# A second seven-product chunk in the first half of both output products of a decoder layer

## The chip, the cores and the metric

The kernel runs on one core of one Trainium2 chip. The metric is device time in microseconds (us) from start to end of the program. Engines are called PE (TensorE, the matmuls), DVE (VectorE), ACT (ScalarE), POOL (GpSimd) and SP (SyncE, which issues most of the transfers). Each of them runs its own list of instructions in the order of that list and waits where an operand is not there yet.

## The reference

One decoder layer on 256 tokens of width 2048, all in float32:

```python
h = h + 0.5 * swiglu(rmsnorm(h, g_ffn1), w1_gate, w1_up, w1_down)
z = rmsnorm(h, g_mix) @ w_in
y_a = spatial_gating(z[..., :2048], g_v, w_s, b_s)          # 1024 channels
y_b = window_attention_sinks(q, k, v, sinks)                # 1024 channels
y = concat(rmsnorm(y_a, g_a_out), rmsnorm(y_b, g_b_out))
h = h + y @ w_out
h = h + cross_attention(rmsnorm(h, g_x), rmsnorm(mem, g_mem), w_xq, w_xkv, w_xo)   # 4 heads x 512
h = h + 0.5 * swiglu(rmsnorm(h, g_ffn2), w2_gate, w2_up, w2_down)
out = rmsnorm(h, g_final)
```

The change touches the two output products, `y @ w_out` (called wo) and the last product of the cross attention, with `w_xo` (called xo). Each is (256 x 2048) by (2048 x 2048) and is added into the residual h.

## The kernel before, in words

**Chunks and units.** Every large product is cut into units of eight chunks. A unit makes 256 tokens x 1024 columns; a chunk is 256 of the 2048 rows of the weight, so a chunk is a 2x2 block product: two blocks of 128 tokens by two blocks of 128 rows (A11, A12, A21, A22), times two by two blocks of weight (B11 to B22, 128 x 512 each). wo and xo are two units each, a first half (columns 0 to 1023) and a second half. The eight chunks of a unit stand at places 0 to 7 in the order in which they are computed, and their sums stay in PSUM banks until the unit is done.

**Three matmuls for one product.** Each operand is split into a high and a low part (`split`, L146: ACT casts the high part, L147, and DVE subtracts it for the low part, L148). A product of two blocks is three matmuls: high x high, low x high, high x low. In every chunk but the first and the last of a unit the passes with the low part of the weight stand last (`passes`, L405).

**Kinds.** A plain chunk (N) has four sums of two block products: 24 matmuls, into the banks P2, Q3, R and Q4. A chunk of kind S replaces the eight block products by seven on sums of blocks (a Strassen-Winograd form): 21 matmuls, into P1, P2, Q3, Q5, Q7, Q6 and Q4. For it DVE and ACT make more: sums of the weight's blocks (L337, L340, L341: the tile named ...t), their high and low parts (...th, ...tl), and sums of the activations' blocks with their parts (L226, L231, L232). The tile names are those of the program: in wo, `wow` is a chunk's weight as loaded, `wowh` and `wowl` its two parts, `wot`, `woth`, `wotl` the sums; `yafh`/`yafl` and `ybfh`/`ybfl` are the parts of the activations (pairs 0 to 3 from y_a, 4 to 7 from y_b). In xo the pairs are `xofh`/`xofl`. `KINDS_O` says that pairs 3 and 5 carry the sums too. The extra banks of an S chunk (P1, Q5, Q6, Q7) come from the pool `trp` of four banks, which the transposes of side work use as well; P2, Q3, R and Q4 come from the pool `acc` of four, so that the next unit's P2, Q3, R and Q4 each wait until DVE has added the old one into h (`adds`, L614).

**Who orders the work.** PE's list is fixed by the program text (`PINNED`). DVE's, ACT's and SP's lists come from a scheduler at build time. Weights go through three buffers (`raw`), their parts through two (`wh`, `wl`), the sums through one (`t`, `th`, `tl`). `push` (L494) prepares a chunk's weight before the chunk ahead of it in the text is multiplied.

**Side work.** Smaller work is written as generators that advance by one step about every six matmuls (`side_step`), for example `y_pairs` (transposes that make the pairs of wo) and `attend_memory` (L1296, one per head: transposes of q, scores, softmax, transposes of the probabilities into `xpT`, their parts `xpTs`, and the products `xo` with the values, two per head; each product is split into one pair of xo). Head 2 makes pairs 4 and 5, head 3 makes pairs 6 and 7. When a chunk needs a pair that does not exist yet, `have` runs the side work to the end of that pair at once (`until`), so its instructions stand directly ahead of the chunk in PE's list. While an S chunk's extra banks are in use, from the first to the last S chunk of a unit, side work is held; ahead of the first S chunk `added_unit` makes all eight pairs.

After the last S chunk `early` adds P1, Q5, Q6 and Q7 into h on DVE; after the last chunk `late` adds P2, Q3, R and Q4. From the finished blocks of h the next norm takes its squares, and then its scaled rows and their transposes, in the second half of the same product.

## Time and profile before

| what | value |
|---|---|
| median of 3 runs | 2036.48 us (2033.58 to 2036.55) |
| the profiled execution's own time | 2033.63 us |
| its span, first to last instruction | 2031.9 us |
| granted TensorE clock, mean | 0.999 |
| PE, DVE, ACT busy share | 99%, 91%, 65% |
| wo (first half from 1045.6, second from 1090.8) | to 1134.9 us |
| xo (first half from 1235.8, second from 1293.2) | to 1338.8 us |

Times in views of the trace are microseconds from the start of the span. A matmul with 512 columns is listed with 0.39 us, though the next one starts sooner, since they are pipelined: distances between starts are what counts on PE. Likewise the next instruction on DVE or ACT may start up to 0.1 us before the listed end of the one ahead.

### The profile page before, as it was taken

Reading aid. Unit: us, or ns where it says so; the run is one execution under the profiler, and the core shown is the slowest. Engines: PE = TensorE matmul, PEld = TensorE weight load, DVE = VectorE, ACT = ScalarE, POOL = GpSimd, SP = SyncE. Lnnn points to the kernel's source line nnn. Section 1 sums busy time; section 2 is a strip of 40 time slices with the busy share of each in tenths; the row PEclk is TensorE's granted clock in tenths of the full one; section 3 lists DMA queues with packets and bytes.
Section 4 is the critical chain, followed back from the end, with each engine's and each line's share of the span. In section 5 each row is a group of like instructions: output and inputs, shape, how many; then the busy total and the mean of one; then the engine's idle time right before and its main releaser. Section 6 shows DMA issues by size and latency. Waiting matters only on the chain.

```text
span 2031.9 us, 24271 instructions
## 1 busy us (share of the span) xinstructions
PE 2015.5 (99%) x9203; PEld 1668.8 (82%) x9203; DVE 1853.6 (91%) x1994; ACT 1313.2 (65%) x1460; POOL 34.4 (2%) x57
## 2 busy tenths in 40 slices
PE   9999999999999999999999999999999999999998
PEld 7788888888888888888888888888888888888886
DVE  6999999999999978989879987899999999999998
ACT  7765566567665766755566666676656666676664
POOL 0000000000000010200000000000000000000000
PEclk9999999999999999999999999999999999999999
DMA  8666666666556575544675544556566656665563
GB/s 312 197 206 225 215 218 205 236 209 220 196 191 219 177 252 178 202 166 166 208 227 182 198 160 145 187 187 224 197 239 215 215 205 231 214 219 206 187 228 125
DMA packets 115333, 415.83 MB, mean 205 GB/s; under 512 B 61824, under 2 KB 63888, under 8 KB 68112
## 3 DMA queue, kind: packets, MB, share of 16 engines
q1 hardware_dynamic: 112768, 407.14, 57.6%
q0 software_dynamic: 2016, 6.30, 1.0%
q8 instruction: 72, 1.18, 0.2%
q10 hardware_dynamic: 432, 0.84, 0.1%
q14 instruction: 45, 0.37, 0.1%
HBM read 398.52 MB, written 2.10 MB: 197 GB/s over the span
## 4 chain that ended last, share of the span: by engine, by line
PE 85%; DVE 9%; issue 3%; ACT 2%; DMA 2%; SPq 0%; POOL 0%; POOLq 0%; DVEq 0%; ACTq 0%
PE f1gQ L428 12%; PE f2gQ L428 12%; PE f2dQ L428 6%; PE f1dQ L428 6%; PE f1gP L428 5%; PE f2gP L428 4%; PE xqQ L428 3%; PE f2dP L428 3%; PE f1dP L428 3%; PE woQ L428 2%; PE xoQ L428 2%; PE f2dR L428 2%; PE f1dR L428 2%; DVE f1gwl L148 2%; PE vQ L428 2%
## 5 line engine op out<-in xcount | busy, mean ns | idle before, releaser
L148 DVE TENSOR_TENSOR f1gwl<-f1gw,f1gwh 128x1536 fp32r<-128x1536 f32 (+2 forms) x94 | 181.6, 1934 | 24.5 <-ACT f1gwh L147 23.8
L147 ACT CAST f2gwh<-f2gw 128x1536 fp32r<-128x1536 f32 (+1 forms) x88 | 150.5, 1712 | 66.4 <-PE f2gQ L428 44.9
L148 DVE TENSOR_TENSOR f2gwl<-f2gw,f2gwh 128x1536 fp32r<-128x1536 f32 (+1 forms) x88 | 179.1, 2036 | 8.0 <-ACT f2gwh L147 8.0
L147 ACT CAST f1gwh<-f1gw 128x1536 fp32r<-128x1536 f32 (+2 forms) x94 | 153.1, 1629 | 45.0 <-PE f1gQ L428 19.3
L147 ACT CAST f1gth<-f1gt 128x1024 fp32r<-128x1024 f32 x76 | 79.9, 1051 | 103.1 <-DVE f1gt L337 68.7
L147 ACT CAST f2gth<-f2gt 128x1024 fp32r<-128x1024 f32 x82 | 85.4, 1050 | 64.2 <-DVE f2gt L341 34.0
L428 PE MATMUL f2gQ<-f2gwh,n4fh 128*128 128x512 f32 x317 | 123.8, 390 | 0.6 <-DVE f2gv L587 0.6
L428 PE MATMUL f2gQ<-f2gwh,n4fl 128*128 128x512 f32 x317 | 123.4, 389 | 0.0
L428 PE MATMUL f1gQ<-f1gwh,n1fl 128*128 128x512 f32 x286 | 111.4, 390 | 1.7 <-DVE n1fl L148 1.7
L428 PE MATMUL f1gQ<-f1gwh,n1fh 128*128 128x512 f32 x286 | 111.6, 390 | 0.0
L147 ACT CAST f2dwh<-f2dw 128x2048 fp32r<-128x2048 f32 (+1 forms) x44 | 77.4, 1758 | 47.5 <-PE f2dQ L428 39.5
L147 ACT CAST f1dwh<-f1dw 128x2048 fp32r<-128x2048 f32 (+1 forms) x44 | 77.3, 1757 | 43.7 <-PE f1dQ L428 42.7
L148 DVE TENSOR_TENSOR f1dwl<-f1dw,f1dwh 128x2048 fp32r<-128x2048 f32 (+1 forms) x44 | 92.0, 2092 | 12.0 <-ACT f1dwh L147 11.8
L148 DVE TENSOR_TENSOR f2dwl<-f2dw,f2dwh 128x2048 fp32r<-128x2048 f32 (+1 forms) x44 | 92.0, 2091 | 11.2 <-ACT f2dwh L147 11.1
L148 DVE TENSOR_TENSOR f2gtl<-f2gt,f2gth 128x1024 fp32r<-128x1024 f32 x82 | 99.5, 1218 | 1.0
L428 PE MATMUL f2gQ<-f2gwl,n4fh 128*128 128x512 f32 x317 | 96.7, 389 | 0.0
L148 DVE TENSOR_TENSOR f1gtl<-f1gt,f1gth 128x1024 fp32r<-128x1024 f32 x76 | 92.2, 1216 | 0.5
L428 PE MATMUL f1gQ<-f1gwl,n1fh 128*128 128x512 f32 x286 | 86.9, 389 | 0.0
L428 PEld LDWEIGHTS f2gQ<-f2gwh,n4fh 128*128 128x128 f32 x317 | 59.5, 188 | 13.8 <-DVE f2gv L587 1.6
L428 PEld LDWEIGHTS f2gQ<-f2gwh,n4fl 128*128 128x128 f32 x317 | 59.5, 188 | 12.2
L428 PEld LDWEIGHTS f2gQ<-f2gwl,n4fh 128*128 128x128 f32 x317 | 59.4, 188 | 12.3
L428 PE MATMUL f2gP<-f2gwh,n4fh 128*128 128x512 f32 x176 | 68.6, 390 | 0.0
(824 smaller groups left out, 6072.2 us busy)
## 6 DMA issues: line engine op xcount, KB each, us to landing
f2gw<-in_w_gu SPq DMA_DIRECT2D x88, 1024.0 KB, 4.9
f1gw<-in_w_gu SPq DMA_DIRECT2D x86, 1024.0 KB, 4.8
f1dw<-in_w_down SPq DMA_DIRECT2D x44, 1024.0 KB, 4.8
f2dw<-in_w_down SPq DMA_DIRECT2D x44, 1024.0 KB, 4.8
wow<-in_w_out SPq DMA_DIRECT2D x16, 1024.0 KB, 4.8
xqw<-in_w_xq SPq DMA_DIRECT2D x16, 1024.0 KB, 4.8
xow<-in_w_xo SPq DMA_DIRECT2D x16, 1024.0 KB, 4.8
qw<-in_w_in SPq DMA_DIRECT2D x8, 1024.0 KB, 4.8
```

The costliest lines, as they stand in the source:

```text
L147: nc.scalar.copy(hi, src)
L148: nc.vector.tensor_tensor(lo, src, hi.bitcast(F32), ALU.subtract)
L428: nc.tensor.matmul(self.banks[name], x, y, start=name not in self.begun, stop=self.left[name] == 0)
```

## The change

In the first half of wo and of xo, chunk 3, whose pair carries the sums anyway, becomes a chunk of kind S beside chunk 5, and the chunks stand in other orders: in wo 0, 1, 2, 4, 5, 6, 3, 7 (S at places 4 and 6), in xo 0, 1, 2, 4, 6, 5, 7, 3 (S at places 5 and 7). Before, both had the order 0 to 7 with S at place 5 alone. The second halves stay as they are. Since xo's first half now ends on an S chunk, its `early` runs inside `late`, and the squares of all four blocks come after all adds.

```diff
-    HALVES_O = ("NNNNNSNN", "NNNSNSNN")
+    HALVES_O = {
+        ("wo", 0): ("NNNNSNSN", (0, 1, 2, 4, 5, 6, 3, 7)),
+        ("xo", 0): ("NNNNNSNS", (0, 1, 2, 4, 6, 5, 7, 3)),
+        ("wo", 1): ("NNNSNSNN", range(8)),
+        ("xo", 1): ("NNNSNSNN", range(8)),
+    }
...
-        def early(u):
+        def early(u, at_once=False):
...
-            if on_block is None:
+            if at_once:
+                rest()
+            elif on_block is None:
...
-        def late(u, blocks=range(TB)):
+        def late(u, blocks=range(TB), also=None):
             for name, tb, j in BLOCKS:
                 if tb in blocks:
                     add(hb(tb, j), u[name], tb, j)
-                    if on_block is not None:
+                    if on_block is not None and also is None:
                         on_block(j0 + j, tb)
+            if also is not None:
+                also(u, True)
+                for name, tb, j in BLOCKS:
+                    on_block(j0 + j, tb)
...
     def added_unit(s, w, cb, pairs, on_block):
-        kinds = HALVES_O[cb]
+        kinds, order = HALVES_O[s, cb]
         u = Unit(s, kinds, LATE_O, clear=True)
...
             push(
-                u, i, w[i, cb],
-                lambda i=i: (have(pairs, 7 if i == kinds.index("S") else i), pairs[i])[1],
-                lambda i=i: early(u) if i == kinds.rindex("S") else end(u) if i == last else None,
+                u, i, w[order[i], cb],
+                lambda i=i: (have(pairs, 7 if i == kinds.index("S") else order[i]), pairs[order[i]])[1],
+                lambda i=i: (
+                    end(u, also=early if kinds[last] == "S" else None) if i == last
+                    else early(u) if i == kinds.rindex("S") else None
+                ),
             )
```

The lists of the engines show more than the diff. Three places follow; a row has the line, the operation, what it writes from what it reads (with the tile's number), and its shape.

DVE in the first half of wo, before: the weight splits of places 2 and 3, then the low part of pair 4 (`ybfl_8581`, in two pieces) and the weight split of place 4.

```order
L148 TENSOR_TENSOR wowl_8529<-wow_8527,wowh_8528 128x2048
L148 TENSOR_TENSOR wowl_8559<-wow_8557,wowh_8558 128x2048
L142 SCALAR_TENSOR_TENSOR ybfl_8581<-yb_8575,sm,ybfh_8580 128x256
L337 TENSOR_TENSOR wot_8674<-wow_8670 128x1024
L142 SCALAR_TENSOR_TENSOR ybfl_8581<-yb_8575,sm,ybfh_8580 128x256
L148 TENSOR_TENSOR wowl_8631<-wow_8629,wowh_8630 128x2048
```

The same stretch of DVE's list after the change, down to the low part of pair 5's sums (`ybfl_8600`):

```order
L337 TENSOR_TENSOR wot_8633<-wow_8629 128x1024
L148 TENSOR_TENSOR wowl_8529<-wow_8527,wowh_8528 128x2048
L148 TENSOR_TENSOR wowl_8559<-wow_8557,wowh_8558 128x2048
L340 TENSOR_TENSOR wot_8633<-wot_8633,wow_8629 128x512
L142 SCALAR_TENSOR_TENSOR ybfl_8581<-yb_8575,sm,ybfh_8580 128x256
L341 TENSOR_TENSOR wot_8633<-wot_8633,wow_8629 128x512
L148 TENSOR_TENSOR wotl_8640<-wot_8633,woth_8639 128x1024
L142 SCALAR_TENSOR_TENSOR ybfl_8581<-yb_8575,sm,ybfh_8580 128x256
...
L340 TENSOR_TENSOR wot_8717<-wot_8717,wow_8713 128x512
L148 TENSOR_TENSOR wowl_8684<-wow_8682,wowh_8683 128x2048
L148 TENSOR_TENSOR ybfl_8600<-ybf_8604,ybfh_8599 128x512
```

The sums of the weight at place 4 now stand around the splits of places 2 and 3 and between the two pieces of pair 4's low part, while pair 4 is read one chunk earlier, at place 3. The low part of pair 5's sums stands behind the split of place 5's weight (`wowl_8684`); on ACT its high part stands behind that weight's cast in the same way, as these rows of ACT's list after the change show:

```order
L147 CAST woth_8643<-wot_8633 128x1024
L147 CAST ybfh_8597<-ybr_8601 128x512
L147 CAST wowh_8683<-wow_8682 128x2048
L147 CAST ybfh_8599<-ybf_8604 128x512
L141 ACTIVATE ybfh_8623<-yb_8618,sm 128x256
```

Before, the cast ahead of `ybfh_8599` was that of the S chunk itself, and the chunk that reads the result stood one place later.

DVE at the turn from the first to the second half of wo, after the change. Ahead of these rows stand the adds of P2 and Q5 into h; the last row is the add of Q4, the fourth bank of the pool `acc`, and the weight split ahead of it belongs to place 1 of the second half:

```order
L645 TENSOR_TENSOR h<-h,woz_8784 128x512
L626 SCALAR_TENSOR_TENSOR h<-woQ_1682_8465,h 128x512
L626 SCALAR_TENSOR_TENSOR h<-woR_8466,h 128x512
L646 TENSOR_TENSOR h<-h,woz_8784 128x512
L148 TENSOR_TENSOR wowl_8844<-wow_8842,wowh_8843 128x2048
L626 SCALAR_TENSOR_TENSOR h<-woQ_1684_8467,h 128x512
```

Before, all four of these adds stood ahead of that split.

PE in the first half of xo, before: the last matmul of place 2, head 2's four transposes, then 18 matmuls of place 3 (the first two and the last two shown) and the first of twelve products with the values.

```order
L428 MATMUL xoQ_2007_10090<-xowl_10147,xofh_10006 128x512 x2
L1332 MATMUL xpT_10309<-ident,pr_10223 128x128 x4
L428 MATMUL xoP_2004_10087<-xowh_10241,xofh_10036 128x512
L428 MATMUL xoP_2004_10087<-xowh_10241,xofl_10037 128x512
...
L428 MATMUL xoP_2004_10087<-xowl_10242,xofh_10036 128x512 x2
L169 MATMUL xo_10342<-xpTs_10314,mvh_10230 128x256
L169 MATMUL xo_10342<-xpTs_10315,mvh_10230 128x256
```

The same place after the change:

```order
L428 MATMUL xoQ_2012_10099<-xowl_10156,xofh_10015 128x512 x2
L1346 MATMUL xpT_10318<-ident,pr_10232 128x128 x4
L169 MATMUL xo_10333<-xpTs_10323,mvh_10239 128x256
L169 MATMUL xo_10333<-xpTs_10324,mvh_10239 128x256
...
L428 MATMUL xoP_2009_10096<-xowh_10250,xofh_10346 128x512
L428 MATMUL xoP_2009_10096<-xowh_10250,xofl_10347 128x512
```

The twelve products now stand directly behind the transposes, and place 3, which has become chunk 4, reads their result (`xofh_10346`, `xofl_10347`) directly behind them. For head 3 the same happens once more at place 4 (chunk 6): six matmuls stand between its transposes and its products, which were twelve before, and the chunk that reads the first result follows at once.

## The prediction

> **What bounds the kernel now.** I read the page first, then PE's waits, then the two stretches that the change touches.

> ```profile
> span 2031.9 us, 24271 instructions
> PE 2015.5 (99%) x9203; PEld 1668.8 (82%) x9203; DVE 1853.6 (91%) x1994; ACT 1313.2 (65%) x1460; POOL 34.4 (2%) x57
> ```

> PE is busy for all but 16 us. The waits of PE in the whole trace are few; the longest are these (waiter, line, releaser, total, times, longest):

> ```profile
> PE f1gQ L428 <- DVE n1fl L148: 1.7, 1, 1.7
> PE xoQ L428 <- ACT n4r L266: 1.2, 1, 1.2
> ```

> One of them, 1.2 us, lies in xo. In the windows of the two first halves (length, then busy time of PE, PEld, DVE and ACT) PE never waits at all:

> ```profile
> 1045.00:1091.00 46.00, 46.00 (x214) 38.11 (x213) 36.66 (x42) 28.92 (x35) 0.00 (x0) 1.00 0.64 196
> 1235.00:1293.00 58.00, 58.00 (x314) 49.85 (x312) 46.83 (x59) 37.66 (x56) 0.00 (x0) 1.00 0.38 135
> ```

> So PE sets the time in both: a matmul less is a gain of one distance between starts, and any new wait of PE is a loss in full. DVE and ACT have free time there, but on average only; what counts is when a given tile is ready.

> **What is removed.** PE's rows in wo give the distance and the places where chunks 4 and 5 start:

> ```profile
> 1064.50 0.40 PE L428 MATMUL woP<-wowh,yafl 128*128 128x512 f32 x1
> 1069.76 0.39 PE L428 MATMUL woP<-wowh,ybfh 128*128 128x512 f32 x1
> 1071.35 0.39 PE L428 MATMUL woQ<-wowh,ybfl 128*128 128x512 f32 x1
> 1075.20 0.39 PE L428 MATMUL woP<-wowh,ybfh 128*128 128x512 f32 x1
> 1076.79 0.39 PE L428 MATMUL woQ<-wowh,ybfl 128*128 128x512 f32 x1
> ```

> 1069.76 to 1071.35 are seven distances: 0.227 us each. Two chunks lose three matmuls each (24 become 21): 6 x 0.227 = **1.4 us gained**. Everything else is a question of lateness.

> **wo, place 3: pair 4 is wanted a chunk earlier and made later.** Its second low piece is needed by the fourth matmul of place 3, which starts at 1064.50 above. DVE's list now begins the stretch with the weight sum of place 4, and that weight must have landed. It is issued by SP and lands 6.5 us later (the list of transfers of that window):

> ```profile
> 1051.19 0.53 SPq L358 DMA_DIRECT2D wow<-in_w_out  x1
> wow<-in_w_out SPq DMA_DIRECT2D x1, 1024.0 KB, 6.5
> ```

> SP's list is unchanged, so it lands at 1057.7 again. Behind it DVE has eight instructions up to that piece. Their durations, on DVE before:

> ```profile
> 1056.05 4.49 DVE L148 TENSOR_TENSOR wowl<-wow,wowh 128x2048 fp32r<-128x2048 f32 x2 [2.07 <-ACT wowh L147]
> 1064.07 1.23 DVE L337 TENSOR_TENSOR wot<-wow 128x1024 f32<-128x1024 f32 x1 [2.72 <-DMA wow<-in_w_out]
> 1065.21 0.48 DVE L142 SCALAR_TENSOR_TENSOR ybfl<-yb,sm,ybfh 128x256 fp32r<-128x256 f32 x1
> 1065.60 2.28 DVE L148 TENSOR_TENSOR wowl<-wow,wowh 128x2048 fp32r<-128x2048 f32 x1
> 1069.75 0.69 DVE L341 TENSOR_TENSOR wot<-wot,wow 128x512 f32<-128x512 f32 x1
> 1070.35 1.22 DVE L148 TENSOR_TENSOR wotl<-wot,woth 128x1024 fp32r<-128x1024 f32 x1
> ```

> 1.23 + 2 x 2.28 + 0.69 + 0.48 + 0.69 + 1.22 + 0.48 = 9.35, less seven overlaps of 0.08 (two splits of 2.28 take 4.49): 8.8 us, so the piece is ready at 1066.5. **Place 3 loses 2.0 us.** If the weight landed before 1056.0, DVE could do the first sum in its 2.07 us of idle time, and 0.3 would be left; if DVE's list were late by one more operation of 0.7, 2.7.

> **wo, place 4: the S chunk is one place earlier.** Its eighth matmul is the first that reads the low part of pair 5's sums; by the rows above it comes 1.59 us after the chunk's start (1075.20 to 1076.79). Place 4 would start at 1069.76 + 2.0 = 1071.8, so it is due at 1073.4. On ACT the high part now stands behind a full weight cast, which waits until PE has left place 3's weight:

> ```profile
> 1061.28 1.91 ACT L147 CAST wowh<-wow 128x2048 fp32r<-128x2048 f32 x1 [0.45 <-PE woQ L428]
> 1068.14 1.49 ACT L147 CAST wowh<-wow 128x1536 fp32r<-128x1536 f32 x1 [1.25 <-PE woQ L428]
> ```

> PE released it at 1068.14; with the 2.0 that is 1070.1, and the cast ends at 1072.0. DVE then has the split of the same weight (2.28, to 1074.3) and the low part of 512 columns (0.69): 1074.95. **Place 4 loses 1.6 us.** It is 0 if the order on ACT costs nothing, and 2.5 if DVE starts 0.9 later.

> **wo, turn to the second half: the fourth bank.** The second half starts here (PE), and DVE added Q4 and split the next weight thus:

> ```profile
> 1090.84 0.39 PE L428 MATMUL woP<-wowh,yafh 128*128 128x512 f32 x1
> 1091.04 0.69 DVE L621 SCALAR_TENSOR_TENSOR h<-woQ,h 128x512 f32<-128x512 f32 x1 [0.67 <-PE woQ L428]
> 1092.96 2.29 DVE L148 TENSOR_TENSOR wowl<-wow,wowh 128x2048 fp32r<-128x2048 f32 x1 [1.23 <-ACT wowh L147]
> ```

> With U the start of the second half, PE wants the Q4 bank after 18 matmuls, at U + 4.1. The add of Q4 now stands behind that split. The split waits for a cast of 1.91 that can start when PE leaves place 7's weight, at about U: it runs from U + 1.9 to U + 4.2, and the add ends at U + 4.9. **0.8 us lost**, between 0 (split elsewhere) and 1.5. The first half of wo thus costs 2.0 + 1.6 + 0.8 = 4.4 us.

> **xo, head 2: its products lose their cover.** PE, then DVE, then ACT, before:

> ```profile
> 1259.92 0.60 PE L1332 MATMUL xpT<-ident,pr 128*128 128x128 f32 x4
> 1260.27 0.48 PE L428 MATMUL xoP<-xowh,xofh 128*128 128x512 f32 x1
> 1264.48 1.59 PE L169 MATMUL xo<-xpTs,mvh 128*128 128x256 f32 x12
> 1265.91 0.63 PE L428 MATMUL xoQ<-xowl,xofh 128*128 128x512 f32 x2
> ...
> 1260.48 2.28 DVE L148 TENSOR_TENSOR xowl<-xow,xowh 128x2048 fp32r<-128x2048 f32 x1
> 1262.76 0.67 DVE L148 TENSOR_TENSOR xpTs<-xpT,xpTs 128x512 fp32r<-128x512 f32 x1
> 1263.87 2.35 DVE L148 TENSOR_TENSOR xotl<-xot,xoth 128x1024 fp32r<-128x1024 f32 x2
> 1266.73 0.69 DVE L148 TENSOR_TENSOR xofl<-xo,xofh 128x512 fp32r<-128x512 f32 x1 [0.51 <-ACT xofh L147]
> ...
> 1261.02 0.58 ACT L147 CAST xpTs<-xpT 128x512 fp32r<-128x512 f32 x1
> 1266.11 0.59 ACT L147 CAST xofh<-xo 128x512 fp32r<-128x512 f32 x1 [0.36 <-PE xo L169]
> 1268.93 0.78 ACT L1359 COPY xor<-xo 128x128 f32<-128x128 f32 x4 [2.23 <-PE xo L169]
> ```

> Up to the transposes nothing has moved. The 4.2 us from 1260.27 to 1264.48 were 18 matmuls of place 3, behind which the split of the probabilities was hidden. Now the products follow at 1260.27. The second of them, 0.12 later (twelve take 1.43 to the next start), reads the low part, which DVE ends at 1262.76 + 0.67 = 1263.43: **3.0 us lost**.

> The group ends 1.47 later, at 1264.9; ACT casts to 1265.5, DVE is in its two sums until 1266.2 (1263.87 + 2.35) and has the low part at 1266.8. The second matmul of place 3 would have started at 1265.0: **1.85 us lost**. Both rest on durations and positions that the trace has almost unchanged; I bound them by 2.4 to 3.2 and 1.2 to 2.2.

> **xo, head 3.** PE goes on with five matmuls, the second product of head 2 (1.43), twelve matmuls, four transposes (0.35) and six matmuls: head 3's second product is due at 1266.8 + 23 x 0.227 + 1.43 + 0.35 + 0.12 = 1273.9. On ACT, head 2's second product (over at 1269.5) starts a chain: four copies (0.78), a cast (0.6), a low part (0.69) and a difference on DVE and a second cast (1.5 together, an estimate from the 0.69 and the casts of 0.6), which is 1272.4; then the S chunk's weight cast (1.49 above), to 1273.8; then the high part (0.58). DVE splits that weight (1.76 for 1536 columns, by 2.28 x 3/4 an estimate of 1.7), to 1275.5, and ends the low part at 1276.2: **2.2 us lost**. The group ends at 1277.6, the cast at 1278.2, the low part at 1278.9, against 1277.7 for the second matmul of place 4: **1.2 us lost**. Bounds: 1.0 to 3.0 and 0.6 to 1.6. The first half of xo costs 3.0 + 1.85 + 2.2 + 1.2 = 8.3 us.

> **Behind the first halves.** The squares for the next norm come later by some adds of 0.69, and the 1.2 us wait of xo's second half can grow by as much or vanish, since PE is late too. I take 0 and keep 1.2 either way. The second matmul after a wait is late too, as after the longest wait of the trace:

> ```profile
> 67.96 0.50 PE L428 MATMUL f1gQ<-f1gwh,n1fl 128*128 128x512 f32 x1 [1.69 <-DVE n1fl L148]
> 68.30 0.39 PE L428 MATMUL f1gQ<-f1gwl,n1fh 128*128 128x512 f32 x1
> 66.00:70.00 4.00, 2.31 (x13) 1.74 (x12) 4.00 (x8) 3.17 (x7) 0.00 (x0) 1.00 0.49 141
> ```

> 0.34 instead of 0.227: 0.1 for each of seven waits, 0.7. The added DVE and ACT work itself (a S chunk's two sums of 1.2 and more) costs nothing beyond these waits, because DVE is busy for 36.66 of 46 us and 46.83 of 58.

> **Sum.** -1.4 + 4.4 + 8.3 + 0.7 = **+12.0 us**. The profiled execution took 2033.63 us with its span of 2031.9; its sum is 2045.6. The median of the runs lies 2.85 above it at 2036.48: I predict **2048.5 us**, 0.6% slower. The bounds together: 0.3 to 2.7, 0 to 2.5 and 0 to 1.5 in wo, 5.2 to 10.0 in xo, 1.2 either way behind. As DVE's lateness at place 3 and at place 4 partly stand in for each other, I let the parts of wo sum to 2 to 6: from 2 + 5.2 - 1.4 - 1.2 = 4.6 to 6 + 10 - 1.4 + 1.2 + 0.7 = 16.5.

> **Rivals.** *Only xo waits.* The transfer of place 4's weight lands before 1056, DVE's idle 2.07 us take the first sum, and place 3 and 4 of wo keep their time: -1.4 + 0.8 + 8.3 + 0.5 = 8.2, 2044.7 us. Against it: the same transfer, behind the same transposes on SP, took 6.5 us. Chance 0.12.

> *The clock falls.* A wait of 3.0 us is longer than any in this trace. If PE came back at half its pace, for as long as at the start of the program, each such wait would cost more:

> ```profile
> 1.12 4.78 PE L98 MATMUL warm<-ones 128*128 128x128 f32 x22 [1.12 <-DVE ones L89]
> ```

> 22 matmuls take 0.21 us each there, where four transposes of the same shape take 0.35 in all (0.09 each). Half pace for 4.8 us loses 2.4 us; for one or two of the four long waits that makes 2051 to 2053.3 us. Against it stands the wait of 1.69 us above: the granted clock of its window is 1.00. Chance 0.08. [...]

> *PE finds everything ready (the other side).* It decides at xo's place 3: if the first group of products starts within 0.5 us of its transposes, the split of the probabilities is done by other means than DVE's list shows, and the rest of the lateness falls with it. Then only the six matmuls and perhaps the 1.2 us wait are gone: 2033.9 to 2035.1 us. For it speaks that DVE is free 9 us of 46 and 11 of 58; against it, that DVE's split of 2.28 starts at 1260.48, just as the transposes end, and stands ahead of the low part. Chance 0.09, 0.01 of it for a change that doesn't take effect (PE would still have its six matmuls).

> **How the numbers follow.** Forecast 0.71; only xo 0.12; clock 0.08; nothing waits 0.09. The forecast's own range is 2041 to 2053 (4.6 to 16.5 over the median). The range to hold the time 8 times in 10 is **2040 to 2054**: it takes in the first rival and most of the second. A measurement of this kernel tells 0.2%, 4.1 us, from no change. Slower by more: 0.71 + 0.12 + 0.08, less 0.03 for a sum near its low bound: 0.88. Faster by more would need 4.1 us, and only 1.4 + 1.2 can be had: 0.02. Same: 0.10.

> **What would show it.** In the profile after, PE's waits should list `xo` (L169) waiting for DVE's `xpTs` twice, 3.0 and 2.2 us, `xoP` for `xofl` twice (1.85 and 1.2), `woP` for `ybfl` (2.0), `woQ` for `ybfl` (1.6) and a `woQ` of the second half for the add of Q4 (0.8); PE should have six matmuls fewer. If xo's products start on time, the forecast is wrong in its largest part; if wo's window shows no wait, the first rival holds; if the window behind the 3.0 us wait has a granted clock below 1.00, the second does.

## The result, and the profile after

The changed kernel takes 2062.1 us (median of four runs, 2061.55 to 2062.68) against 2035.75 us of the kernel before on the same chip. The ratio is 1.0135, with a 95% interval of 1.0123 to 1.0147: 1.35% slower. The forecast was 2048.5 us with a range of 2040 to 2054. The direction was right; the loss is more than twice the 12.0 us of the forecast, and outside the range. The profiled execution took 2062.68 us, its span 2060.7 against 2031.9: 28.8 us are to be found. (That is more than the 26.35 between the medians, since the profiled execution before was among the fastest of its kernel.)

The engines on the page of the changed kernel (busy time, share of the span, instructions):

```profile
PE 2025.7 (98%) x9197; PEld 1673.1 (81%) x9197; DVE 1862.1 (90%) x2004; ACT 1316.1 (64%) x1464; POOL 37.9 (2%) x57
```

PE has its six matmuls less (9203 to 9197). Its busy time grew all the same, by 10 us, which waits alone do not explain. The windows of the two first halves, which PE filled completely before (length, then busy time of PE, PEld, DVE, ACT and POOL, the granted clock, the share of the DMA engines, GB/s):

```profile
1045.00:1091.00 46.00, 40.02 (x174) 31.81 (x173) 31.49 (x35) 27.56 (x31) 0.00 (x0) 0.93 0.52 161
1235.00:1293.00 58.00, 51.70 (x273) 43.43 (x273) 40.70 (x54) 34.20 (x55) 0.00 (x0) 0.94 0.33 118
```

So there are new waits, and the granted clock, 1.00 before, is 0.93 and 0.94. PE's waits in the whole trace (waiter, line, releaser, total, times, longest). Left out are those which the kernel before has too, among them 1.7 us for `n1fl` and the wait for `f2gv`, which grew from 0.6 to 1.8 us:

```profile
PE n L248 <- ACT n4s L848: 4.4, 1, 4.4
PE xo L169 <- DVE xpTs L148: 3.2, 2, 1.7
PE woQ L428 <- DVE ybfl L142: 3.1, 1, 3.1
PE woQ L428 <- DVE ybfl L148: 1.7, 1, 1.7
PE xo L169 <- ACT xpTs L147: 1.5, 2, 1.1
PE f2gQ L428 <- ACT f2gth L147: 1.4, 1, 1.4
PE xoP L428 <- ACT xofh L147: 1.4, 2, 0.7
PE woP L428 <- DVE ybfl L142: 1.1, 1, 1.1
PE woQ L428 <- DVE h L626: 0.7, 1, 0.7
```

The waits for `xpTs`, for `xofh` (the same places where the forecast named `xofl`), `woP` for `ybfl`, `woQ` for `ybfl` of L148 and `woQ` for the add into `h` are the forecast's. Two of the longest are not: `woQ` for `ybfl` of L142 (3.1) and the transposes `n` for `n4s` (4.4). The wait of `xoQ` for `n4r` (1.2) is gone.

Next, a count of my own over PE's rows: of each distance between two starts, what exceeds the median distance of that form of matmul, as long as it is over 0.06 us; where the granted clock is 0.5, up to one median of it is put down to the clock. In us, before and after:

| stage (us of the changed kernel's span) | waits before | waits after | half clock after |
|---|---|---|---|
| up to 1040 | 20.4 | 19.5 | 0 |
| wo, 1040 to 1120 | 0.8 | 8.7 | 2.05 |
| xq, 1120 to 1240 | 1.2 | 1.7 | 0 |
| xo's first half, 1240 to 1300 | 0.5 | 9.0 | 2.5 |
| turn in xo, n4, 1300 to 1345 | 1.8 | 5.05 | 2.3 |
| start of the last feed-forward part, to 1420 | 0.9 | 2.35 | 0 |
| the rest | 2.1 | 4.0 | 0 |

The differences add up to 29.6, less 1.4 for six matmuls: 28.2 of the 28.8. Half clock, 6.9 us in all, is a quarter of the loss.

**The bank in wo.** PE in place 4 (start, duration, engine, line, operation, tiles, count, in brackets the idle time before it and who ended it), then DVE and ACT there:

```profile
1074.12 0.50 PE L428 MATMUL woQ<-wowh,ybfl 128*128 128x512 f32 x1 [1.70 <-DVE ybfl L148]
...
1074.91 0.40 PE L428 MATMUL woQ<-woth,ybfl 128*128 128x512 f32 x1
1078.46 0.76 PE L428 MATMUL woQ<-woth,ybfh 128*128 128x512 f32 x1 [3.15 <-DVE ybfl L142]
1079.02 0.63 PE L428 MATMUL woQ<-woth,ybfl 128*128 128x512 f32 x1
1079.45 0.63 PE L428 MATMUL woQ<-woth,ybfh 128*128 128x512 f32 x1
...
1076.16 1.76 DVE L148 TENSOR_TENSOR wowl<-wow,wowh 128x1536 fp32r<-128x1536 f32 x1 [0.71 <-ACT wowh L147]
1077.83 0.87 DVE L142 SCALAR_TENSOR_TENSOR ybfl<-yb,sm,ybfh 128x256 fp32r<-128x256 f32 x2
...
1074.65 1.47 ACT L147 CAST wowh<-wow 128x1536 fp32r<-128x1536 f32 x1 [2.42 <-PE woQ L428]
1076.03 0.83 ACT L141 ACTIVATE ybfh<-yb,sm 128x256 fp32r<-128x256 f32 x2
```

The matmul at 1078.46 is the first into another bank of the chunk of seven. It does not read the `ybfl` that released it (those are the low parts of pairs 6 and 7, which this chunk does not use): its four additional banks come from the pool of four in which the transposes `yb` stand too (L67, L416), and the transposes of these two pairs are read straight from PSUM by L141 and L142. In the program as built, this matmul, the first into Q7, waits for the second low piece of pair 6, and the first into Q6 for that of pair 7. These second pieces stand behind the cast (1074.65) and the split (1076.16) of the weight of place 6, the second chunk of seven, and that cast waited until PE had got past its earlier wait, at 1074.12. One wait has made the next. Behind it the matmuls come every 0.43 us, not every 0.227.

**n4s.** The chain that PE's longest wait ends, on DVE, POOL and ACT:

```profile
1317.33 2.29 DVE L148 TENSOR_TENSOR xowl<-xow,xowh 128x2048 fp32r<-128x2048 f32 x1
1319.53 0.15 DVE L126 TENSOR_REDUCE ss<-parts 128x2 f32<-128x4 f32 x1
1319.59 1.21 DVE L337 TENSOR_TENSOR xot<-xow 128x1024 f32<-128x1024 f32 x1
1320.73 0.16 DVE L130 TENSOR_SCALAR ms<-ss 128x2 f32<-128x2 f32 x1
1320.79 2.28 DVE L148 TENSOR_TENSOR xowl<-xow,xowh 128x2048 fp32r<-128x2048 f32 x1
1323.00 0.68 DVE L340 TENSOR_TENSOR xot<-xot,xow 128x512 f32<-128x512 f32 x1
1323.60 1.22 DVE L148 TENSOR_TENSOR xotl<-xot,xoth 128x1024 fp32r<-128x1024 f32 x1
1324.73 0.68 DVE L341 TENSOR_TENSOR xot<-xot,xow 128x512 f32<-128x512 f32 x1
...
1320.97 5.00 POOL L132 TENSOR_TENSOR rs<-ms,mhalf 128x2 f32<-128x2 f32 x1 [171.96 <-DVE ms L130]
...
1326.00 2.56 ACT L848 ACTIVATE n4s<-h,rs 128x512 f32<-128x512 f32 x4 [4.11 <-POOL rs L132]
```

The last squares come when all adds are done, their sum stands behind a split of 2.29 us, the mean behind 1.21 us more, and the power of two columns on POOL takes 5.00 us. Before, it took 1.11 (DVE, then POOL):

```profile
1298.87 0.69 DVE L340 TENSOR_TENSOR xot<-xot,xow 128x512 f32<-128x512 f32 x1
1299.00 1.11 POOL L132 TENSOR_TENSOR rs<-ms,mhalf 128x2 f32<-128x2 f32 x1 [159.29 <-DVE ms L130]
```

### The profile page after: what moved, and what is told of

Read it like the earlier page. It is cut to its first block, busy times and chain, and to the rows that moved or that the text cites. A ratio compares the mean times of both kernels' runs of the same rounds, so it can differ in the third digit from the quotient of the medians.

```text
span 2060.7 us, 24280 instructions
## 1 busy us (share of the span) xinstructions
PE 2025.7 (98%) x9197; PEld 1673.1 (81%) x9197; DVE 1862.1 (90%) x2004; ACT 1316.1 (64%) x1464; POOL 37.9 (2%) x57
## 4 chain that ended last, share of the span: by engine, by line
PE 79%; issue 11%; DVE 8%; ACT 1%; POOL 0%; DMA 0%; POOLq 0%; DVEq 0%; ACTq 0%
PE f2gQ L428 15%; PE f1gQ L428 12%; PE f2dQ L428 6%; PE f1dQ L428 6%; PE f2gP L428 5%; PE f1gP L428 5%; PE f2dP L428 3%; PE f1dP L428 3%; PE f2dR L428 2%; PE f1dR L428 2%; DVE f1gwl L148 2%; PE woQ L428 2%; PE vQ L428 2%; PE mv0Q L428 2%; PE mv1Q L428 1%
## 5 line engine op out<-in xcount | busy, mean ns | idle before, releaser
L148 DVE TENSOR_TENSOR f1gwl<-f1gw,f1gwh 128x1536 fp32r<-128x1536 f32 (+2 forms) x94 | 181.7, 1934 | 23.6 <-ACT f1gwh L147 22.6
L147 ACT CAST f2gwh<-f2gw 128x1536 fp32r<-128x1536 f32 (+1 forms) x88 | 150.2, 1711 | 63.1 <-PE f2gQ L428 43.5
L148 DVE TENSOR_TENSOR f2gwl<-f2gw,f2gwh 128x1536 fp32r<-128x1536 f32 (+1 forms) x88 | 179.2, 2037 | 10.5 <-ACT f2gwh L147 10.4
L147 ACT CAST f1gwh<-f1gw 128x1536 fp32r<-128x1536 f32 (+2 forms) x94 | 153.1, 1629 | 45.2 <-PE f1gQ L428 17.9
L147 ACT CAST f1gth<-f1gt 128x1024 fp32r<-128x1024 f32 x76 | 79.9, 1052 | 102.7 <-DVE f1gt L337 67.7
L147 ACT CAST f2gth<-f2gt 128x1024 fp32r<-128x1024 f32 x82 | 85.7, 1049 | 70.5 <-DVE f2gt L341 35.1
L428 PE MATMUL f2gQ<-f2gwh,n4fh 128*128 128x512 f32 x317 | 124.1, 391 | 1.8 <-DVE f2gv L592 1.8
L428 PE MATMUL f2gQ<-f2gwh,n4fl 128*128 128x512 f32 x317 | 123.4, 389 | 0.0
L428 PE MATMUL f1gQ<-f1gwh,n1fl 128*128 128x512 f32 x286 | 111.4, 390 | 1.7 <-DVE n1fl L148 1.7
L428 PE MATMUL f1gQ<-f1gwh,n1fh 128*128 128x512 f32 x286 | 111.6, 390 | 0.0
L147 ACT CAST f2dwh<-f2dw 128x2048 fp32r<-128x2048 f32 (+1 forms) x44 | 77.3, 1758 | 47.4 <-PE f2dQ L428 39.8
L147 ACT CAST f1dwh<-f1dw 128x2048 fp32r<-128x2048 f32 (+1 forms) x44 | 77.3, 1757 | 43.7 <-PE f1dQ L428 39.5
L148 DVE TENSOR_TENSOR f1dwl<-f1dw,f1dwh 128x2048 fp32r<-128x2048 f32 (+1 forms) x44 | 92.1, 2093 | 12.0 <-ACT f1dwh L147 11.8
L148 DVE TENSOR_TENSOR f2dwl<-f2dw,f2dwh 128x2048 fp32r<-128x2048 f32 (+1 forms) x44 | 92.0, 2092 | 11.2 <-ACT f2dwh L147 10.9
L148 DVE TENSOR_TENSOR f2gtl<-f2gt,f2gth 128x1024 fp32r<-128x1024 f32 x82 | 99.8, 1219 | 1.0
L428 PE MATMUL f2gQ<-f2gwl,n4fh 128*128 128x512 f32 x317 | 96.7, 389 | 0.0
L148 DVE TENSOR_TENSOR f1gtl<-f1gt,f1gth 128x1024 fp32r<-128x1024 f32 x76 | 92.3, 1218 | 0.5
L428 PE MATMUL f1gQ<-f1gwl,n1fh 128*128 128x512 f32 x286 | 86.9, 389 | 0.0
L428 PEld LDWEIGHTS f2gQ<-f2gwh,n4fh 128*128 128x128 f32 x317 | 59.5, 188 | 16.0 <-DVE f2gv L592 3.9
L428 PEld LDWEIGHTS f2gQ<-f2gwl,n4fh 128*128 128x128 f32 x317 | 59.4, 188 | 12.4
L428 PEld LDWEIGHTS f2gQ<-f2gwh,n4fl 128*128 128x128 f32 x317 | 59.5, 188 | 12.1
L428 PE MATMUL f2gP<-f2gwh,n4fh 128*128 128x512 f32 x176 | 68.6, 390 | 0.0
## 6 DMA issues: line engine op xcount, KB each, us to landing
f2gw<-in_w_gu SPq DMA_DIRECT2D x88, 1024.0 KB, 4.9
f1gw<-in_w_gu SPq DMA_DIRECT2D x86, 1024.0 KB, 4.9
f1dw<-in_w_down SPq DMA_DIRECT2D x44, 1024.0 KB, 4.8
f2dw<-in_w_down SPq DMA_DIRECT2D x44, 1024.0 KB, 4.8
wow<-in_w_out SPq DMA_DIRECT2D x16, 1024.0 KB, 4.8
xqw<-in_w_xq SPq DMA_DIRECT2D x16, 1024.0 KB, 4.8
xow<-in_w_xo SPq DMA_DIRECT2D x16, 1024.0 KB, 4.8
qw<-in_w_in SPq DMA_DIRECT2D x8, 1024.0 KB, 4.8
```

What stands on the lines that cost most here:

```text
L147: nc.scalar.copy(hi, src)
L148: nc.vector.tensor_tensor(lo, src, hi.bitcast(F32), ALU.subtract)
L428: nc.tensor.matmul(self.banks[name], x, y, start=name not in self.begun, stop=self.left[name] == 0)
```

## Experiments

My theory T from these rows: the new orders make tiles late (not the second chunk of seven by itself); in wo the late pairs also hold a bank, at xo's end the chunk of seven at the last place makes `n4s` late, and the clock is halved behind each cluster of waits (0.5 for 6.83 us in each of the three places). Each run was timed beside the kernel before; ratios are to that, with 95% intervals. The edits are to the changed kernel unless the text says otherwise.

### Each of the two products alone

```diff
-        ("xo", 0): ("NNNNNSNS", (0, 1, 2, 4, 6, 5, 7, 3)),
+        ("xo", 0): ("NNNNNSNN", range(8)),
```

> Only the first half of wo is changed; xo keeps its order and its one chunk of seven products. Theory T (the loss of wo is its own, as the changed kernel's trace has it): up to the second half of wo PE falls 9.4 us behind the kernel before (waits of 1.7, 1.9 and 3.3 us, about 2 us of matmuls at 427 ns behind the last of them, 0.9 at the turn), and xo then costs nothing: +9.4, about 2045.2 us. Rival R (the prediction's terms: 2.0 + 1.6 + 0.8 + 0.3 - 0.7): +4.0, about 2039.8 us. Rival C (the two places only hurt each other: a late wo makes xo late): under +2 us.

1.0051 (1.0036 to 1.0066): 10.4 us, near T's 9.4 and far from the prediction's terms (4.0). xo, as before, has no new wait.

```diff
-        ("wo", 0): ("NNNNSNSN", (0, 1, 2, 4, 5, 6, 3, 7)),
+        ("wo", 0): ("NNNNNSNN", range(8)),
```

> Only the first half of xo is changed; wo stays as before. Theory T: +16 us up to the end of xo and +3.5 at the start of the last feed-forward part, 19.4 in all, about 2055 us; PE waits 4 to 5 us for n4s. Rival R (the prediction's terms: 3.0 + 1.85 + 2.2 + 1.2 + 0.4 - 0.7): +8.0, about 2043.7 us. Rival C: the sum of the two runs' losses falls 3 us or more short of the 26.3 us of the whole change, because a part of xo's loss comes from wo.

1.0100 (1.0085 to 1.0115): 20.3 us, T's 19.4. The two sum to 30.7, against 27.5 for the whole change by its ratio. So the places don't share a loss (rival C). That the sum lies 3.2 us above it is within the intervals, 3 us to either side for each of the two runs. By my count it is the clock: xo's half clock costs 8.8 us here and 4.8 in the whole change, with waits that are the same to 0.2 us. Why that can differ stands in the last section.

### The order without the second chunk of seven

```diff
-        ("wo", 0): ("NNNNSNSN", (0, 1, 2, 4, 5, 6, 3, 7)),
-        ("xo", 0): ("NNNNNSNS", (0, 1, 2, 4, 6, 5, 7, 3)),
+        ("wo", 0): ("NNNNSNNN", (0, 1, 2, 4, 5, 6, 3, 7)),
+        ("xo", 0): ("NNNNNSNN", (0, 1, 2, 4, 6, 5, 7, 3)),
```

> The new orders of chunks alone: chunk 3 goes to its new place but stays a chunk of eight products, so there is one chunk of seven in each first half as before (place 4 in wo, place 5 in xo). Theory T (the order makes tiles late, and the chunk of seven at the last place of xo makes the wait for n4s): wo loses 10 us (its chunk of seven is still at place 4, so the wait for a PSUM bank stays), xo about 10 (both heads), the wait for n4s and what follows it is gone: +20, about 2056 us. Rival W (the added chunks' weight sums and splits on DVE make the lateness): most of it goes, +2 to +6, 2038 to 2042 us.

1.0118 (1.0103 to 1.0133): 24 us of the 27.5. Rival W (2038 to 2042) falls. The waits of this kernel:

```profile
PE woQ L428 <- DVE ybfl L142: 3.7, 1, 3.7
PE xo L169 <- DVE xpTs L148: 3.5, 2, 2.1
PE woQ L428 <- DVE ybfl L148: 1.5, 1, 1.5
PE xoQ L428 <- ACT n4r L266: 1.2, 1, 1.2
```

wo's and the heads' waits stay, the wait for `n4s` is gone and the 1.2 for `n4r` is back, as T has it. T's 2056 was 2.5 too low: the half clock of xo's first half takes 6.5 us here, not 2.5. The wait for `f2gth` (1.4) is gone too, and it is there in every run with two chunks of seven in xo's first half; how they make it wasn't followed up.

### What holds the power on POOL

The copy makes DVE wait for the power, so that DVE has a gap:

```diff
                     st["est"] = rstd_of(parts[:, :, :2], 2, 1024)
+                    if s == "n4":
+                        seen = tiny.tile([P, TB], F32, tag="seen", name=nm("seen"), bufs=1)
+                        with tc.high_priority():
+                            nc.vector.tensor_copy(seen, st["est"])
```

> The changed kernel, with one copy of 2 columns on DVE that reads the power on POOL (rs, 5.0 us in the changed kernel, 0.7 to 1.1 elsewhere) which n4s waits for; it stands behind the split of xowl (2.28 us) that follows the mean, so DVE has nothing to do from that split's end until the power is there. Theory P (POOL gets through only when DVE isn't busy with operations that read two tiles): the power ends within 1 us of that split's end, 2.6 to 3.3 us after its start instead of 5.0, the wait for n4s shrinks by about 2 us, the total by 2 to 3: about 2059.5 us. Rival S (POOL is slow there for a reason of its own): 5.0 us again, the copy waits for it, 2062 us.

2059.4 us, 1.0126 (1.0109 to 1.0143). Beside the changed kernel's 1.0135 that difference is too small for the runs; the span is 3.1 us shorter, the wait for `n4s` 2.4 instead of 4.4, and the half clock behind it is gone. What decides is POOL (POOL, then DVE):

```profile
1323.16 2.66 POOL L132 TENSOR_TENSOR rs<-ms,mhalf 128x2 f32<-128x2 f32 x1 [173.27 <-DVE ms L130]
1322.98 2.28 DVE L148 TENSOR_TENSOR xowl<-xow,xowh 128x2048 fp32r<-128x2048 f32 x1
1325.85 0.17 DVE L838 COPY seen<-rs 128x2 f32<-128x2 f32 x1 [0.58 <-POOL rs L132]
```

The power takes 2.66 us and ends 0.56 us behind the end of the split (1325.26 to 1325.82). In the changed kernel it ended at 1325.97, 0.56 behind the last of four operations without a gap between them (1324.73 + 0.68 = 1325.41), and in the kernel before 0.55 behind L340 (1299.56 to 1300.11). With DVE pausing behind the split (0.58 us), the power ended 0.56 us behind the split, in the time that theory P gives. Rival S falls. That POOL needs such a pause is not shown, and other rows speak against it (last section).

### Chunks of seven at places 5 and 6

```diff
-        ("wo", 0): ("NNNNSNSN", (0, 1, 2, 4, 5, 6, 3, 7)),
-        ("xo", 0): ("NNNNNSNS", (0, 1, 2, 4, 6, 5, 7, 3)),
+        ("wo", 0): ("NNNNNSSN", (0, 1, 2, 4, 6, 5, 3, 7)),
+        ("xo", 0): ("NNNNNSSN", (0, 1, 2, 4, 6, 5, 3, 7)),
```

> The changed kernel with the two chunks of seven at places 5 and 6 of both first halves (order 0, 1, 2, 4, 6, 5, 3, 7). Theory T (in wo the bank is held by pairs 6 and 7, which at place 4 are not made yet; in xo the wait for n4s comes of a chunk of seven at the last place): the wait of 3.1 us in wo and the half clock behind it go, and so does the wait for n4s with the half clock behind it (5.6 us in all); both heads of xo stay as they are. Total 8 to 10 us below the changed kernel, 2052 to 2054. Rival B (pairs 6 and 7 are late wherever they are wanted first): wo loses 9 to 10 us as before and only the n4s part goes, 2056 to 2057.

1.0120 (1.0105 to 1.0135), 2058.8 us: neither number. What T says of the two places is borne out: there is no wait for a bank that a pair holds, and between 1320 and 1332 PE is busy all 12 us at a granted clock of 1.00, without a wait for `n4s`. (The wait for the fourth bank at the turn stays, 1.0 us in wo, and xo has one of 1.0 too.) But in wo the lateness came out elsewhere (`woP` waits three times for `ybfl`, 3.0 us in all, as pair 4 is wanted at place 3 and pair 6 at place 4; 7.1 us of waits in wo by my count, against 8.7), and the half clock of xo's first half grew from 2.5 to 5.2. For wo, rival B was nearer.

### PE kept busy where it waits

Matmuls of a zero matrix, into a bank in use, ahead of the two waits of wo's place 4 (`zero` is made once at the start). They add work and add zero to the bank:

```diff
             for n, (name, x, y) in enumerate(steps):
+                if self.s == "wo" and self.kinds[6] == "S" and chunks_done.get("wo") == 4 and n in (7, 11):
+                    for _ in range(7 if n == 7 else 12):
+                        nc.tensor.matmul(self.banks["P2"], zero, steps[0][2], start=False, stop=False)
```

> The changed kernel with matmuls of a zero matrix added in wo, place 4, each adding nothing to a bank in use: 7 ahead of the 1.9 us wait (1.6 us of work) and 12 ahead of the 3.3 us wait (2.7 us), so that PE works where it waited. Theory H (PE's clock is halved by the share of idle time in fixed stretches of 3.41 us): no half clock in wo, the matmuls behind the wait take 227 ns and not 427, PE starts the second half of wo 2 us earlier, total about 2060. Rival D (the matmuls are slow there for another reason, for instance the DMA at a share of 0.7 and the weights it brings): 427 ns stay, total 2062 or more.

1.0129 (1.0114 to 1.0144), and a span of 2059.0 us, 1.7 less with 19 matmuls more; the ratio alone couldn't tell that from nothing. The same stretches of 3.41 us, in the changed kernel and then with the added matmuls:

```profile
1072.19:1075.60 3.41, 1.42 (x5) 0.67 (x4) 3.26 (x5) 0.99 (x2) 0.00 (x0) 1.00 0.27 62
1075.60:1079.01 3.41, 0.55 (x1) 0.50 (x2) 2.54 (x3) 1.26 (x3) 0.00 (x0) 0.50 0.68 262
1079.01:1082.42 3.41, 3.41 (x9) 2.64 (x8) 0.10 (x1) 2.03 (x2) 0.00 (x0) 0.50 0.77 291
```

```profile
1072.19:1075.60 3.41, 3.37 (x15) 2.43 (x14) 3.41 (x6) 1.03 (x3) 0.00 (x0) 1.00 0.24 50
1075.60:1079.01 3.41, 3.41 (x17) 2.74 (x16) 0.76 (x2) 0.75 (x1) 0.00 (x0) 1.00 0.61 257
1079.01:1082.42 3.41, 3.41 (x17) 2.81 (x16) 2.65 (x2) 2.63 (x3) 0.00 (x0) 1.00 0.02 5
```

Full clock throughout, 17 matmuls where there were 9. Between 1075.6 and 1079.0 the DMA engines move as much as in the changed kernel (0.61 and 0.68), so rival D falls. With PE busy for 3.37 us of the first stretch in place of 1.42, the granted clock behind it was 1.00 in place of 0.50. The changed kernel itself has both opposites of rival D: half clock from 1276.98 to 1280.40 with a DMA share of 0.00, and full clock from 1061.95 to 1065.36 with one of 1.00.

### Two chunks of seven without a new order

```diff
-    KINDS_O = "NNNSNSNN"
+    KINDS_O = "NNNNNSSN"
     HALVES_O = {
-        ("wo", 0): ("NNNNSNSN", (0, 1, 2, 4, 5, 6, 3, 7)),
-        ("xo", 0): ("NNNNNSNS", (0, 1, 2, 4, 6, 5, 7, 3)),
-        ("wo", 1): ("NNNSNSNN", range(8)),
-        ("xo", 1): ("NNNSNSNN", range(8)),
+        ("wo", 0): ("NNNNNSSN", range(8)),
+        ("xo", 0): ("NNNNNSSN", range(8)),
+        ("wo", 1): ("NNNNNSSN", range(8)),
+        ("xo", 1): ("NNNNNSSN", range(8)),
```

> Two chunks of seven in the first halves without any new order: chunks 5 and 6 are of that kind, at places 5 and 6, in both halves of wo and xo, chunk 3 has eight products again. PE has the same six matmuls fewer. Theory T (the order makes the tiles late, not the second chunk of seven): heads 2 and 3 of xo keep their cover and pair 4 of wo its place, so there is no wait over 1.5 us that the kernel before doesn't have, and no half clock: 2034 to 2040 us. Rival W (the second chunk's sums, casts and splits make DVE and ACT late wherever it stands): waits of 2 us and more in both first halves, 2044 us or more.

1.0062 (1.0047 to 1.0077), 2046.3 us: T's price is wrong, and the time is rival W's. For xo T's places are right: the heads have their cover (1.2 us of waits from 1240 to 1300, against 9.0), and nothing in wo or xo runs at half clock (granted 1.00 in both). So W's waits of 2 us and more in both first halves aren't there. But PE now waits for the splits of weights: `woP` twice for `wowl`, 1.3 us in wo's first half and 2.2 at the start of its second, and `f2gP` twice for `f2gwl`, 2.6 us in all. What makes these late wasn't followed up. It needn't be that one chunk of seven stands straight behind the other, since the run with both at places 5 and 6 of the first halves has no wait for `wowl`. This run also moves chunks of seven in the second halves, so these 12 us are not the price of the first halves alone.

### wo's pairs earlier

The table YFORMS says how many chunks must be done before each pair of wo may be made:

```diff
-    YFORMS = (9, 10, 11, 16, 16, 17, 17, 18)
+    YFORMS = (9, 10, 11, 14, 14, 15, 15, 16)
```

> The changed kernel with pairs 3 to 7 of wo allowed two chunks earlier (14, 14, 15, 15, 16 chunks done in place of 16, 16, 17, 17, 18), so that their parts stand further ahead in the lists of PE, ACT and DVE. Theory T (only lateness costs wo, DVE and ACT have the time): the waits of wo's first half fall from 7.9 us to under 3, no half clock there, total 7 to 9 us below the changed kernel, 2053 to 2055. Rival K (the work is only moved: the chunks of the memory's keys ahead of wo lose as much): 2060 to 2063.

1.0090 (1.0073 to 1.0107), 2052.3 us: about 9 us less than the changed kernel by the ratios. wo's waits fall to 1.7 us by my count, and its first half is full again at full clock:

```profile
1045.00:1091.00 46.00, 46.00 (x212) 38.13 (x211) 38.97 (x44) 29.08 (x30) 0.00 (x0) 1.00 0.68 207
```

The same with xo as before,

```diff
-        ("xo", 0): ("NNNNNSNS", (0, 1, 2, 4, 6, 5, 7, 3)),
+        ("xo", 0): ("NNNNNSNN", range(8)),
...
-    YFORMS = (9, 10, 11, 16, 16, 17, 17, 18)
+    YFORMS = (9, 10, 11, 14, 14, 15, 15, 16)
```

> The new order and the second chunk of seven in wo alone, xo as before, and pairs 3 to 7 of wo allowed two chunks earlier as in the run before. Theory T (wo's whole loss of 9.4 us is lateness of the pairs and the half clock that follows it): with the pairs earlier wo has under 2 us of waits, full clock and three matmuls fewer, and nothing else is changed: 2033 to 2036 us, within 0.2% of the kernel before. Rival M (a part of the gain of the run before came from xo, where the half clock took 1.5 us less): wo still loses 3 us or more, 2037 us and above.

0.9999 (0.9989 to 1.0009): the whole loss of wo is gone, to within 2 us. And the YFORMS edit alone, in the kernel before:

> The kernel before with nothing but pairs 3 to 7 of wo allowed two chunks earlier, to see whether that alone is a gain or a loss. Theory T (the kernel before waits 0.8 us in all in wo, so nothing can be gained, and the chunks ahead of wo have the time on DVE and ACT): 2033 to 2036 us. Rival K (the work taken ahead costs cover in the memory's keys): 2037 us or more.

0.9998 (0.9989 to 1.0008). The earlier pairs are neither gain nor loss in themselves; they cure lateness that the new order made.

### xo's heads

```diff
-        yield 4
+        yield 3
         ps = bank("xs")
...
-        yield 5
+        yield 4
         ptv = bank("xpT")
```

> The changed kernel with the heads' steps one step closer to each other (3 and 4 in place of 4 and 5), so that between the transposes of head 2 and its first product PE has 12 matmuls of xo and the 24 of head 3's scores again, as it had 18 matmuls in the kernel before. Head 3 keeps its six matmuls between the two. Theory T (head 2's 3.0 us is cover that the order took away): PE waits under 0.5 us for head 2's xpTs, pair 4's split still costs 1.5 to 2, head 3's waits stay, and the half clock behind head 2 goes or moves: 2056.5 to 2059 us. Rival S (the scores of head 3 stand too close to their inputs and wait in their turn): 2060.5 us or more.

1.0140 (1.0123 to 1.0157), 2061.6 us: rival S. The waits for `xpTs` of head 2 are gone, but others stand in their place: `xs` waits 2.2 us in all for `mkl`, and `xoP` 2.0 for `xofl`. xo's first half waits 9.3 us, where it waited 9.0. Its half clock is gone (2.5 us), which with 1.0 us more waits in xq leaves nearly nothing. A last run has this edit, the YFORMS edit and xo's chunks of seven at places 5 and 6 (`("xo", 0): ("NNNNNSSN", (0, 1, 2, 4, 6, 5, 3, 7))`):

> The changed kernel with the three cures together: pairs 3 to 7 of wo two chunks earlier, the heads' steps closer, and xo's chunks of seven at places 5 and 6 instead of 5 and 7. Theory T (the losses are separate latenesses that add): 9.8 us from wo, 3 to 5 from head 2, 5 from n4s and its half clock: 2042 to 2045 us. Rival S (what one cure takes away another wait or the half clock takes back): 2047 us or more.

1.0087 (1.0072 to 1.0102), 2051.7 us: rival S again, no better than the YFORMS edit alone. xo's first half still waits 10.8 us. With xo's order the one edit that was tried in its heads doesn't recover the time. I read this so: the heads' chain is late as a whole when pair 4 is wanted a chunk earlier, and a wait that is taken from one step turns up at the next. No run shows that by itself, so for xo's heads the order is shown as the cause, but no cure was found.

## Why the prediction was right in sign and wrong in size

**The terms that it had** came out well. In us, forecast and measured (from PE's starts: when the matmul in question came, and when it would have come at median distances):

| step | forecast | measured |
|---|---|---|
| six matmuls | -1.4 | -1.4 |
| wo, place 3 | 2.0 | 1.8 |
| wo, place 4 | 1.6 | 1.9 |
| wo, turn (fourth bank) | 0.8 | 0.8 |
| xo, head 2 | 3.0 | 3.1 |
| pair 4's split | 1.85 | 1.5 |
| xo, head 3 | 2.2 | 2.6 |
| pair 6's split | 1.2 | 1.3 |

For head 2, for example:

```profile
1269.11 0.60 PE L1346 MATMUL xpT<-ident,pr 128*128 128x128 f32 x4
1270.84 0.39 PE L169 MATMUL xo<-xpTs,mvh 128*128 128x256 f32 x1 [1.13 <-ACT xpTs L147]
1272.67 2.00 PE L169 MATMUL xo<-xpTs,mvh 128*128 128x256 f32 x11 [1.45 <-DVE xpTs L148]
```

The second product was due 0.47 us after the transposes' start, at 1269.58; it came 3.1 later. The seven losses sum to 13.0 against 12.65. That these waits come from the order is shown by the orders alone (24 us) and by two chunks of seven without a new order (no wait in the heads). Rivals one and three, in which PE waits less or not at all, fall with the waits for `ybfl` and `xpTs`.

**"Place 4 loses 1.6 us" stopped one step short.** I followed the chunk of seven to its eighth matmul and pair 5's sums, not to its other needs: four banks of a pool that the last pairs' transposes still hold. That cost 3.3 us (1074.91 to 1078.46, less one distance), more than any term of the sum. I listed what is queued behind the late weight for pair 5 and not for pairs 6 and 7, whose second pieces stand behind the weight of place 6 in the same lists. With pairs 3 to 7 earlier the wait is gone along with the others.

**"Behind the first halves ... I take 0"** was the second step that failed. I priced the later adds and not what follows them: with the chunk of seven at the last place the adds, the squares, their sum, the mean and the power come in a row, behind two weight operations (2.29 and 1.21), and the power itself grew from 1.1 to 5.0 us. PE's transposes came 4.6 us late; less the 1.2 for `n4r` that this made go, 3.4. The orders without the last chunk of seven, and the chunks at places 5 and 6, don't have this wait; with DVE's pause of 0.58 us it falls from 4.4 to 2.4.

**The rival that the clock falls** (chance 0.08, 2051 to 2053.3) was right in kind, and it joined the forecast rather than take its place. Its price was 2.4 us for one or two waits; it was 2.05, 2.5 and 2.3 in three places. I gave it little because the wait of 1.69 us had full clock and my longest was 3.0; that it takes a single wait longer than that was an assumption, which no run shows. Waits of 1.9 and 3.3 us with four matmuls between them were enough: of the 3.41 us from 1072.19 on PE was busy for 1.42, and the granted clock behind them was 0.50.

**The resumption** (0.1 per wait) holds: 0.34 us instead of 0.227 after the wait at 1074.12. **The rest**: the wait for `f2gth` (1.6 with the start behind it) and small waits in the last feed-forward part (about 2) were not foreseen; the runs don't settle where they come from.

13.0 - 1.4 + 3.3 + 3.4 + 6.9 + 1.6 = 26.8 of 28.8; the rest is the slower matmul behind each wait and those small waits. (0.35 of the 1.5 for pair 4's split is half clock, which the 6.9 has too.) The range failed because it took its bounds from the terms that I had. It had no room for a place that I had not priced, and I had let the two losses that I did have, clock and lateness, exclude each other.

## What to carry to other kernels

When a step of an in-order program is moved forward, list everything that it needs (operands, the buffers and PSUM banks that it writes, and who must let go of these), not just the operand that is late first, and do the same at the far end for what is computed when it is over. Sum the waits of PE that lie close together, too: here half clock cost another 2.05, 2.5 and 2.3 us behind three clusters of them, and of the 3.41 us ahead of each half clock PE had been busy for 1.42, 1.29 and 1.00. Before a shorter piece of work is bought with a new order, look whether the tiles can be made earlier: here a table of start conditions gave back the 10 us that the new order had cost in wo, and the 0.7 us of matmuls saved there were too little to show.

## What the runs showed of the hardware

```profile
1061.95:1065.36 3.41, 2.27 (x12) 1.35 (x10) 3.41 (x7) 2.21 (x5) 0.00 (x0) 1.00 1.00 420
1283.81:1287.23 3.42, 1.99 (x10) 1.19 (x7) 2.40 (x3) 1.96 (x3) 0.00 (x0) 1.00 0.00 0
```

and the one with 1.42 above had half clock behind it. Of the stretches at half clock, all 25 in which PE was busy for 3.24 us or more had full clock behind them, and none of the 19 with 3.00 or less. The same waits in xo lay differently on these stretches in the changed kernel and in the run with xo alone. In the stretch in which head 3's waits begin PE was busy for 1.99 us in the changed kernel (1283.81 above), and for 1.71 in the other run (from 1274.93), where half clock followed for 10.24 us. That is how I read the 4.8 and 8.8 us of half clock; no run moved the position by itself.

**A power of 128x2 on POOL took 0.69 to 5.00 us.** In the fourteen executions, up to the final norm, 64 powers began while DVE ran no operation with two operands; they took 0.69 to 0.72 us (nine of them in the kernel before and the changed kernel, 0.69 to 0.71). The other 90 began while it ran one, and each ended 0.55 to 0.59 us behind the end of such an operation. For 85 that was the operation that ran at the start, and most of them took 0.9 to 1.1 us (the twelve of the same two kernels 0.89 to 1.14). For five, all of them this power behind a chunk of seven at xo's last place, it was the third operation after that, and they took 5.00 us. Why it ended only behind the third in these five stays open. That there is no gap between them doesn't explain it: in wo DVE went on without a gap too, and the power ended 0.55 us behind the first operation, as in 13 more of the 85 (POOL, then DVE):

```profile
1105.21 1.12 POOL L132 TENSOR_TENSOR rs<-ms,mhalf 128x2 f32<-128x2 f32 x1 [137.61 <-DVE ms L130]
1105.09 0.69 DVE L341 TENSOR_TENSOR wot<-wot,wow 128x512 f32<-128x512 f32 x1
1105.70 1.22 DVE L148 TENSOR_TENSOR wotl<-wot,woth 128x1024 fp32r<-128x1024 f32 x1
```
